# Second attention of an encoder layer: value loads that wait for an exponential, transposes called earlier, thirteen units without copies

## The chip, the cores and the metric

The kernel runs on one core of one Trainium2 chip. The metric is the device time of one execution in microseconds (us). Times before the change are the median of three runs and one profiled execution of the same program.

## The reference: one encoder layer on two sequences

Two sequences of 2048 tokens and width 1024 go through one layer with shared weights. An input projection yields queries, keys, values and gates of two attention branches. Branch A is windowed attention (8 query heads, 2 key heads). Branch B, which the change touches, is neighbourhood attention: the tokens form a grid of 32 rows by 64 columns, and each query sees a window of 8 rows by 16 columns. Both are gated, concatenated, projected out and added to the input, and a gated side path is added. Cut to branch B:

```python
def neighbourhood_attn(q, k, v, rpb):
    ...
    def row(r):
        ...
        sc = jnp.einsum('bnqhd,banchd->bnhqac', qr, kb).astype(jnp.float32) * scale
        ...
        sc = jnp.where(mask, sc + bias.astype(jnp.float32), -jnp.inf)
        sc = sc.reshape(b, NA_N_COL_BLOCKS, B_HEADS, NA_COL_BLOCK, wr * NA_KEY_COLS)
        pr = jax.nn.softmax(sc, axis=-1)
        pr = pr.reshape(b, NA_N_COL_BLOCKS, B_HEADS, NA_COL_BLOCK, wr, NA_KEY_COLS).astype(vb.dtype)
        o = jnp.einsum('bnhqac,banchd->bnqhd', pr, vb)
        return o.reshape(b, GRID_W, B_WIDTH)
```

## The kernel before

Products that need accuracy split each fp32 operand into a high and a low part of type fp32r and run three matmuls (`project`: high x high, high x low, low x high).

**Stages.** The program has 96 units `f`. Units 0 to 31 are the tiles of branch A. Units 32 to 95 are branch B: `divmod` splits `f - 32` into a half of the heads (32 to 63 and 64 to 95), a sequence and a tile `j` of 16, which is a block of 8 grid rows `b` and of 16 columns `cb`. Its 128 queries see 288, 384, 360 or 480 keys, by `j`, in 3 or 4 chunks (`window`, `chunks`); units with `j` = 5, 6, 9, 10 are the wide ones (480 keys, 4 chunks), those with `j` = 0, 3, 12, 15 the narrow ones (288). After unit 95 follow the output projection and the side path.

**What TensorE does in a unit.** Beside the attention of unit `f` run the projections of a tile six ahead (`stream`, `proj_b`: pqk for queries and keys, pvg for values and gates, 24 matmuls each, at 215 ns by the planner's count, 10320 a unit). The table `PLAN_B` says at which share of the unit's projection each step of the attention is called: the four score products (`sc`, tile scb), the exponentials (`exp`), the preparation of the next queries (`prep`), four times the transposes (`pt`, tile ptb), and four times the product with the values (`po`, tile pob), of which the last two are called in the next unit (second number 0). The order on TensorE is pinned to the order of the calls; on the other engines and on SP's queue a scheduler orders the instructions, unless `P` pins them.

**The way of the exponentials.** DVE adds the bias to the scores and takes the maximum (`softmax`, s, mx), ACT takes the exponential in place in the order of heads 0, 2, 1, 3 (`exps`). The transposes are cheaper in fp32r. So a DMA on ACT's queue copies each head's exponentials from s to tn, a tile of type fp32r (L310), and `pt` transposes tn. If `exps` gets no tile `turned`, there is no copy and `pt` transposes s as fp32. Before, the last six units (90 to 95) do that. The transposed probabilities are split into high and low part by ACT (p_t, L935) and DVE (L936); the products pob go through an addition otb (ACT L954, DVE L955) to the output.

**Loads on SP's queue.** SP issues its DMAs in order. In each unit these are the values vw (`load_values`, three or four loads, L903, called with `exp`), the store of the output (ob_d, L964), the biases of the next unit that has new ones (L888), stores of projected values (v_d, L846) and the next tokens (stx, L361). In units 56 and 57 SP also loads the weights of the second half of heads (wa and wb, eight times 512 KB each, L197), in units 88 and 89 the first weights of the next stage (L1013). The biases wait for the last exponential of the unit before (`last_ex`, through `after`). The scratch buffers that the steps share are small rings: `sc` (3 PSUM banks, for scores, transposes and gates), s (5) and p_t (3).

Of the kernel before, what the change touches and what calls it, by code (L numbers as in the profile page):

```python
# [11 lines left out]
F32 = mybir.dt.float32  # L12
# [46 lines left out]
def bias_offsets():  # L59
# [39 lines left out]
PLAN_B = (  # L99
    (0.00, 1, "sc", 0), (0.03, 1, "sc", 1), (0.07, 1, "sc", 2), (0.09, 0, "po", 2), (0.11, 1, "sc", 3), (0.16, 0, "po", 3),  # L100
    (0.16, 1, "exp", 0), (0.24, 0, "fin", 0), (0.35, 1, "prep", 0),
    (0.68, 1, "pt", 0), (0.75, 1, "pt", 1), (0.82, 1, "pt", 2), (0.86, 1, "po", 0), (0.90, 1, "pt", 3), (0.95, 1, "po", 1),
)


def emit(ctx, tc, io):
# [179 lines left out]
    def after(ins, other):  # L286

        tc.add_manual_dep(ins.ins, other.name, mybir.DependencyInfo(mybir.DependencyClass.Sync, mybir.DependencyReason.DATA),
                          reason="behind the copies")

    def exps(sm, fct, gs, sink=None, turned=None):

        mx, nm, den, rd, ss = (sm[k] for k in ("mx", "nm", "den", "rd", "s"))
        if sink is None:
            nc.vector.tensor_scalar_mul(nm, mx, -1.0)
            yield
        else:
            nc.vector.scalar_tensor_tensor(out=nm, in0=mx, scalar=-1.0, in1=sink[1], op0=ALU.mult, op1=ALU.min)  # L298
        waiting = []
        for n_, i in enumerate((0, 2, 1, 3) if sink is None else range(4)):  # L300
            ex = nc.scalar.activation(ss[i], ss[i], AF.Exp, bias=nm[:, i:i + 1], accum_out=den[:, i:i + 1])  # L301
            if sink is None:
                last_ex[:] = [ex.ins]
            if sink is None and (n_ == 0 or turned is not None):
                P(ex)
            if sink is None and turned is not None:
                waiting.append(i)
                for k in waiting[:1] if n_ in (1, 2) else waiting[:] if n_ == 3 else ():
                    to = turned[:, k, :ss[k].shape[-1]]
                    P(nc.scalar.dma_start(to.bitcast(F32), ss[k]))  # L310
                    ss[k] = to
                    waiting.remove(k)
        if sink is not None:
            es = ap.tile([128, 4], F32, tag="es", name="es", bufs=3)
            nc.vector.tensor_tensor(out=es, in0=sink[0], in1=nm, op=ALU.add)
            nc.scalar.activation(es, es, AF.Exp)
            yield
            behind(nc.vector.tensor_tensor(out=den, in0=den, in1=es, op=ALU.add))
            nc.vector.reciprocal(out=nm, in_=den)
            nc.gpsimd.tensor_copy(rd, nm)  # L320
            nc.gpsimd.tensor_copy(rd[0:64, 1::2], nm[64:128, 0::2])
            nc.gpsimd.tensor_copy(rd[64:128, 0::2], nm[0:64, 1::2])
        else:
            nc.vector.reciprocal(out=rd, in_=den)
        nc.gpsimd.tensor_scalar_mul(rd, rd, fct)
        g2 = ap.tile([128, 4, HD], F32, tag="g2", name="g2", bufs=2)
        nc.gpsimd.tensor_tensor(out=g2, in0=gs.rearrange("p (h d) -> p h d", h=4),
                                in1=rd.unsqueeze(2).broadcast_to([128, 4, HD]), op=ALU.mult)
        sm["g2"] = g2.rearrange("p h d -> p (h d)")
        yield  # L330
# [540 lines left out]

    bt = []

    def unit_b(f):
        half, st = divmod(f - 2 * NT, 2 * NT)
        s, j = divmod(st, NT)
        b, cb = divmod(j, 4)
        _, gs = held[f]
        r0, nr, c0, ncol, rows = window(b, cb)
        kc, ch = rows * ncol, chunks(nr, rows)  # L880
        nch, kn = len(ch), [ncol * n for _, n in ch]
        n = nr * ncol
        if cb != 2:
            off, _ = BIAS_OFF[(row_type(b), col_type(cb))]
            if not bt:
                bt.append(big([128, 2, 4, 512], F32, "bias"))
            bt.append(bt[0][:, len(bt) % 2])
            load = nc.sync.dma_start(bt[-1][:, :, :n],  # L888
                                     io["bias"][half][:, off:off + 4 * n].rearrange("p (h n) -> p h n", h=4))
            if last_ex:  # L890
                after(load, last_ex[0])
        bias = bt[-1]
        vw = []

        def load_values():

            spare = f >= 6 * NT - 6 and f % 2 == 0
            if spare:
                four = ap.tile([128, 4, 4, 2 * HD], F32R, tag="raw", name="vw4", bufs=1)
            for j in range(nch):  # L900
                v = four[:, j] if spare else \
                    ap.tile([128, 4, 2 * HD], F32R, tag=("vp", "vr_")[j % 2], name="vw", bufs=3 - j % 2)
                nc.sync.dma_start(v[:kn[j]].bitcast(F32).rearrange("p h d -> p (h d)"),  # L903
                                  v_d[half, s, cb][r0 + ch[j][0]:r0 + sum(ch[j])]
                                  .rearrange("r c h a d -> (r c) (h a d)"))
                vw.append(v)

        sees = [query_rows(b, cb, j) for j in range(nch)]
        order = sorted(range(nch), key=lambda j: sees[j][1] - sees[j][0])
        at = [16 * sum(z - a for a, z in sees[:j]) for j in range(nch + 1)]  # L910
        sm, p_ts, got = sm_tiles(), [], {}

        def sc(h):
            ps = ptile([128, 512], "sc", "scb")
            for j, q in enumerate(qs[f]):
                mm(ps[:, :n].rearrange("p (r c) -> p r c", c=ncol), q[h % 2][:, 128 * (h // 2):128 * (h // 2) + 128],
                   ks_b[h % 2][:, r0:r0 + nr, h // 2, c0:c0 + ncol], j == 0, j == 1)
            softmax(h, ps, n, bias[:, h, :n], sm)
            if h == 3:
                if not tn:  # L920
                    tn.append(ap.tile([128, 4, 480], F32R, tag="ev", name="tn", bufs=1))
                got["ex"] = exps(sm, hr_b[:, st:st + 1], gs, turned=tn[0] if f < 6 * NT - AHEAD - 1 else None)
                next(got["ex"])

        def pt(x):
            h = (0, 2, 1, 3)[x]
            pt = ptile([128, 512], "pt", "ptb")
            for j in order:

                c = at[j] - 16 * sees[j][0]  # L930
                k0 = ncol * ch[j][0]
                tr(pt[:kc, c:c + 128], sm["s"][h][:, k0:k0 + kc], rowwise)
            p_t = main.tile([128, 2, 512], F32R, tag="p_t", name="p_t", bufs=3)
            hi, lo, pf = p_t[:kc, 0, :at[-1]], p_t[:kc, 1, :at[-1]], pt[:kc, :at[-1]]
            nc.scalar.copy(hi, pf)  # L935
            nc.vector.tensor_tensor(out=lo, in0=pf, in1=hi.bitcast(F32), op=ALU.subtract)  # L936
            p_ts.append(p_t)

        def po(x):
            h = (0, 2, 1, 3)[x]  # L940
            e, i = h % 2, h // 2
            if i == 0:
                got["po"] = ptile([128, 2, 256], "ms", "pob")
            if x == 0:
                got["ot"] = ap.tile([128, 2, 2, 128], F32, tag="ot", name="otb", bufs=2)
            po, ot = got["po"], got["ot"]
            for j in order[::-1]:
                a, z = sees[j]
                mm(po[:, i, :].rearrange("p (a q) -> p a q", a=2)[:, :, 16 * a:16 * z], vw[j][:kn[j], h, :],
                   p_ts[x][:kn[j], :, at[j]:at[j + 1]], j == order[-1], j == order[0])  # L950
            if i == 1:
                a, z = 64 * e, 64 - 64 * e
                pq = po.rearrange("p i (a q) -> p i a q", a=2)
                nc.scalar.copy(ot[a:a + 64], pq[z:z + 64])  # L954
                nc.vector.tensor_tensor(out=ot[a:a + 64], in0=pq[a:a + 64], in1=ot[a:a + 64], op=ALU.add)  # L955

        def fin(_):
            pgt = ptile([128, 2, 128], "sc", "pgtb")
            for i in range(2):
                tr(pgt[:, i, :], sm["g2"][:, 128 * i:128 * i + 128], rowwise)  # L960
            o_t = ap.tile([128, 2, 128], F32, tag="o_t", name="o_tb", bufs=2)
            nc.gpsimd.tensor_tensor(out=o_t, in0=got["ot"][:, :, 0], in1=got["ot"][:, :, 1], op=ALU.add)
            nc.vector.tensor_tensor(out=o_t, in0=pgt, in1=o_t, op=ALU.mult)
            nc.sync.dma_start(ob_d[s][b, :, 2 * half:2 * half + 2, cb, :], o_t)  # L964
        return {"sc": sc, "pt": pt, "po": po, "fin": fin, "prep": lambda _: nxt(f),
                "exp": lambda _: (next(got["ex"]), load_values())}


# [500 lines left out]
```

## Time and profile before

| what | us |
|---|---|
| median of three runs | 2490.5 (2489.25 to 2492.84) |
| the profiled execution | 2492.04 |
| its span, first to last instruction | 2490.3 |
| first attention, 0 to 806.70 | 806.70, TensorE busy 793.95 |
| second attention, units 32 to 89, 806.70 to 1757.45 | 950.75, TensorE busy 928.56 |
| units 90 to 95, 1757.45 to 1841.00 | 83.55, TensorE busy 81.58 |
| output projection and side path, 1841.00 to the end | 649.30, TensorE busy 643.39 |

The page gives shares of the span by engine. In its second part the digits are tenths of busy time in 40 slices of the span; the DMA line is the mean busy share of the core's 16 DMA engines.

```profile
PEclk9999999999999999999999999999999999999999
DMA  6422233322354677767967787777977455756765
GB/s 208 134 97 94 88 103 98 97 94 87 102 178 153 203 252 234 232 210 228 336 217 228 225 266 255 244 247 266 316 232 272 163 171 175 265 176 217 242 227 170
```

Slices are 62.3 us wide. In the second attention (slices 13 to 28) the DMA engines are busy between 60% and over 90%; the highest rate, 336 GB/s, falls on the slice from 1183 to 1245 us, in units 55 to 58. In the third part, q1 is SP's queue and q10 is ACT's, which carries hardly anything but the copies to tn:

```profile
q1 hardware_dynamic: 245376, 437.84, 54.1%
q10 hardware_dynamic: 33696, 45.09, 5.3%
```

### The profile page before, as it was taken

What the parts mean: (1) busy time and instruction counts of PE and PEld (TensorE: products, weight loads), DVE (VectorE), ACT (ScalarE), POOL (GpSimd) and SP (SyncE); (2) the same over time, 40 slices, a digit from 0 to 9 for tenths busy, and PEclk for the clock granted to TensorE, in tenths of its full rate; (3) what the DMA queues carried; (4) which work ended last, traced back from release to release, by engine and by line L of the source; (5) the groups of instructions that cost most, each with busy time, mean ns of one, the idle gap of its engine ahead of it and who ended that gap; (6) DMA issues with size and microseconds to landing.
All of it is one profiled execution on the core that took longest, in us unless ns stands there. A gap on an engine that the chain in (4) does not pass through costs nothing. (4 is left out here: it accounts for less than half of the span.)

```text
span 2490.3 us, 40934 instructions
## 1 busy us (share of the span) xinstructions
PE 2447.5 (98%) x13062; PEld 2060.5 (83%) x13062; DVE 1705.6 (68%) x4215; ACT 1412.8 (57%) x3408; POOL 853.1 (34%) x1363
## 2 busy tenths in 40 slices
PE   8999999999999999999899999999999999999999
PEld 7888888888888888888778888887777888888887
DVE  6777777777765666666566666776537655686776
ACT  6777777777764665665456566665663222354443
POOL 4555555555543544554344444443110000000000
PEclk9999999999999999999999999999999999999999
DMA  6422233322354677767967787777977455756765
GB/s 208 134 97 94 88 103 98 97 94 87 102 178 153 203 252 234 232 210 228 336 217 228 225 266 255 244 247 266 316 232 272 163 171 175 265 176 217 242 227 170
DMA packets 279288, 485.55 MB, mean 195 GB/s; under 512 B 31617, under 2 KB 120097, under 8 KB 274849
## 3 DMA queue, kind: packets, MB, share of 16 engines
q1 hardware_dynamic: 245376, 437.84, 54.1%
q10 hardware_dynamic: 33696, 45.09, 5.3%
q8 instruction: 104, 1.70, 0.3%
q14 instruction: 112, 0.91, 0.1%
HBM read 307.72 MB, written 134.23 MB: 177 GB/s over the span
## 5 line engine op out<-in xcount | busy, mean ns | idle before, releaser
L258 PE MATMUL pqk<-wa,xr 128*128 128x512 f32 x1536 | 452.5, 411 | 0.0
L258 PE MATMUL pvg<-wb,xr 128*128 128x512 f32 x1536 | 450.6, 406 | 0.0
L301 ACT ACTIVATE s<-s,nm 128x320 f32<-128x320 f32 (+6 forms) x512 | 293.5, 575 | 131.1 <-DVE nm L298 119.1
L258 PEld LDWEIGHTS pvg<-wb,xr 128*128 128x128 f32 x1536 | 272.5, 190 | 34.1
L1254 ACT CAST opd<-raw 128x512 fp32r<-128x512 f32 x224 | 131.7, 619 | 270.6 <-PE acca L1272 117.9
L258 PEld LDWEIGHTS pqk<-wa,xr 128*128 128x128 f32 x1536 | 257.1, 188 | 29.7
L379 POOL TENSOR_TENSOR xr<-stx,xr 128x512 fp32r<-128x512 f32 x186 | 238.6, 1296 | 107.5 <-ACT xr L378 77.7
L1255 DVE TENSOR_TENSOR opd<-raw,opd 128x512 fp32r<-128x512 f32 x224 | 146.6, 686 | 145.6 <-ACT opd L1254 145.6
L258 PE MATMUL pg<-wb,xr 128*128 128x512 f32 x768 | 233.0, 409 | 1.0 <-DVE vv L536 1.0
L258 PE MATMUL pq<-wa,xr 128*128 128x512 f32 x768 | 219.3, 400 | 0.0
L954 ACT COPY otb<-pob 64x512 f32<-64x512 f32 x128 | 74.5, 582 | 213.3 <-PE pob L258 213.1
L936 DVE TENSOR_TENSOR p_t<-ptb,p_t 128x368 fp32r<-128x368 f32 (+5 forms) x256 | 121.6, 487 | 91.3 <-ACT p_t L935 88.7
L1272 PE MATMUL accc<-opd,wb 128*128 128x512 f32 x768 | 177.0, 389 | 0.5 <-DVE r L1317 0.5
L1272 PE MATMUL acca<-opd,wa 128*128 128x512 f32 (+1 forms) x780 | 176.2, 386 | 0.8 <-ACT r L1350 0.5
L1272 PE MATMUL acca<-opd,s 128*128 128x512 f32 x768 | 175.4, 389 | 0.0
L1272 PEld LDWEIGHTS acca<-opd,wa 128*128 128x128 f32 x780 | 144.9, 188 | 30.9 <-ACT ev L1050 0.8
L1272 PEld LDWEIGHTS accc<-opd,wb 128*128 128x128 f32 x768 | 144.1, 188 | 30.8 <-DVE r L1317 1.0
L1272 PEld LDWEIGHTS acca<-opd,s 128*128 128x128 f32 x768 | 144.2, 188 | 29.9
L143 POOL TENSOR_TENSOR yb<-vrb,power 128x8 f32<-128x8 f32 x64 | 106.5, 1664 | 175.7 <-DVE vrb L813 158.0
L935 ACT CAST p_t<-ptb 128x368 fp32r<-128x368 f32 (+5 forms) x256 | 107.5, 427 | 86.5 <-PE ptb L262 74.6
L258 PEld LDWEIGHTS pob<-p_t,vw 128*128 128x128 f32 (+2 forms) x832 | 132.6, 189 | 24.6 <-DVE p_t L936 4.4
L258 PEld LDWEIGHTS pq<-wa,xr 128*128 128x128 f32 x768 | 135.1, 189 | 17.3
(174 smaller groups left out, 5188.1 us busy)
## 6 DMA issues: line engine op xcount, KB each, us to landing
stx<-x_b SPq DMA_DIRECT2D x128, 256.0 KB
vw<-v_d SPq DMA_DIRECT2D x96, 256.0 KB
stx<-x_a SPq DMA_DIRECT2D x64, 256.0 KB
stn<-x_n SPq DMA_DIRECT2D x64, 256.0 KB
v_d<-vb SPq DMA_DIRECT2D x64, 256.0 KB
ple_d<-ev SPq DMA_DIRECT2D x64, 256.0 KB
xres<-x_r SPq DMA_DIRECT2D x64, 256.0 KB
x_d<-r SPq DMA_DIRECT2D x64, 256.0 KB
```

The lines of the kernel that those rows point to most:

```text
L143: nc.gpsimd.tensor_tensor(out=y, in0=v, in1=power.broadcast_to([128, n]), op=ALU.pow)
L258: pinned(nc.tensor.matmul(out, lhsT, rhs, start=start, stop=stop))
L301: ex = nc.scalar.activation(ss[i], ss[i], AF.Exp, bias=nm[:, i:i + 1], accum_out=den[:, i:i + 1])
L379: low.tensor_tensor(out=lo, in0=raw, in1=hi.bitcast(F32), op=ALU.subtract)
L935: nc.scalar.copy(hi, pf)
L936: nc.vector.tensor_tensor(out=lo, in0=pf, in1=hi.bitcast(F32), op=ALU.subtract)
L954: nc.scalar.copy(ot[a:a + 64], pq[z:z + 64])
L1254: P(nc.scalar.copy(hi, v))
L1255: P(nc.vector.tensor_tensor(out=lo, in0=v, in1=hi.bitcast(F32), op=ALU.subtract))
L1272: pinned(nc.tensor.matmul(ps[:, cols], w[k][:, a, c:c + 128], o[:, b, cols], start=i in (0, 1, 4) and k == 0 and j == 0, stop=k == 3 and j ...
```

## The change

Four edits. In `PLAN_B` the transposes 0 to 2 are called earlier (0.60, 0.68, 0.76), the last one later (0.94), and the first two products with the values later (0.91 and 0.98). The value loads of a unit that copies wait for that unit's second exponential. A new function `copied_` names the units that copy: all but 55 to 58 and 87 to 95, so that 13 units transpose in fp32 instead of 6. The biases wait for the last exponential of the unit before only if that unit and their own both copy.

```diff
@@ -99,7 +99,7 @@
 PLAN_B = (
     (0.00, 1, "sc", 0), (0.03, 1, "sc", 1), (0.07, 1, "sc", 2), (0.09, 0, "po", 2), (0.11, 1, "sc", 3), (0.16, 0, "po", 3),
     (0.16, 1, "exp", 0), (0.24, 0, "fin", 0), (0.35, 1, "prep", 0),
-    (0.68, 1, "pt", 0), (0.75, 1, "pt", 1), (0.82, 1, "pt", 2), (0.86, 1, "po", 0), (0.90, 1, "pt", 3), (0.95, 1, "po", 1),
+    (0.60, 1, "pt", 0), (0.68, 1, "pt", 1), (0.76, 1, "pt", 2), (0.91, 1, "po", 0), (0.94, 1, "pt", 3), (0.98, 1, "po", 1),
 )
@@ -300,7 +300,7 @@
             if sink is None:
-                last_ex[:] = [ex.ins]
+                last_ex[:] = last_ex[-3:] + [ex.ins]
@@ -871,6 +871,10 @@
+    def copied_(f):
+
+        return not (4 * NT - 9 <= f < 4 * NT - 5 or f >= 6 * NT - 9)
+
@@ -887,8 +891,8 @@
-            if last_ex:
-                after(load, last_ex[0])
+            if f > 2 * NT and copied_(f) and copied_(f - 1):
+                after(load, last_ex[-1])
@@ -900,9 +904,11 @@
-                nc.sync.dma_start(v[:kn[j]].bitcast(F32).rearrange("p h d -> p (h d)"),
+                load = nc.sync.dma_start(v[:kn[j]].bitcast(F32).rearrange("p h d -> p (h d)"),
...
+                if copied_(f):
+                    after(load, last_ex[1])
                 vw.append(v)
@@ -919,7 +925,7 @@
-                got["ex"] = exps(sm, hr_b[:, st:st + 1], gs, turned=tn[0] if f < 6 * NT - AHEAD - 1 else None)
+                got["ex"] = exps(sm, hr_b[:, st:st + 1], gs, turned=tn[0] if copied_(f) else None)
```

On TensorE, in the middle of an ordinary unit (unit 34; pktb are transposes of the keys, pqk the projection, ptb the transposes of the exponentials, x3 one head's), the difference reads:

```order
 L264 MATMUL pktb<-ident,kb 128x128 x2
 L258 MATMUL pqk<-wa_9501,xr 128x512 x3
-L258 MATMUL pqk<-wa_9503,xr 128x512 x3
+L258 MATMUL pqk<-wa_9503,xr 128x512 x2
+L262 MATMUL ptb<-rowwise,tn 128x128 x3
+L258 MATMUL pqk<-wa_9503,xr 128x512
 L258 MATMUL pqk<-wa_9505,xr 128x512 x3
 L262 MATMUL ptb<-rowwise,tn 128x128 x3
 L258 MATMUL pqk<-wa_9507,xr 128x512 x3
+L258 MATMUL pqk<-wa_9509,xr 128x512
 L262 MATMUL ptb<-rowwise,tn 128x128 x3
```

The first head's transposes stand behind 5 products of pqk instead of 9, the second's behind 9 instead of 12, and the third's (not shown) behind 13 instead of 16.

On DVE, from the end of unit 33 to the first softmax of unit 34 (p_t is the low part of the transposed probabilities, ssqb the sum of squares of the projection, otb the addition behind the second product with the values; s,mx the softmax), before:

```order
L936 TENSOR_TENSOR p_t<-ptb,p_t 128x320 x4
L955 TENSOR_TENSOR otb<-pob,otb 64x512
L810 TENSOR_REDUCE ssqb<-sqb 128x8
L277 ISA s,mx<-scb,bias 128x384
L277 ISA mx 128x1
L813 TENSOR_SCALAR vrb<-ssqb,ep_b 128x8
```

and in the changed kernel:

```order
L942 TENSOR_TENSOR p_t<-ptb,p_t 128x320 x3
L810 TENSOR_REDUCE ssqb<-sqb 128x8
L961 TENSOR_TENSOR otb<-pob,otb 64x512
L813 TENSOR_SCALAR vrb<-ssqb,ep_b 128x8
L277 ISA s,mx<-scb,bias 128x384
L277 ISA mx 128x1
```

The addition moves behind the sum of squares, and the first softmax behind both and behind vrb. 16 of the 64 units have this order; in the others the first softmax stands ahead of the addition.

On SP's queue, in unit 56, the end of the weight loads wa and the biases of unit 57 (128x4x480) before:

```order
L197 DMA wa_15570<-sp_1wa_214 128x1024
L197 DMA wa_15572<-sp_1wa_215 128x1024
L197 DMA wa_15574<-sp_1wa_216 128x1024
L197 DMA wa_15576<-sp_1wa_217 128x1024
L888 DMA bias<-bias 128x4x480
L846 DMA v_d_309<-vb 8x8x512
```

and in the changed kernel, where the first two of the eight weight loads are the last rows shown:

```order
L907 DMA vw<-v_d_308 120x512 x2
L892 DMA bias<-bias 128x4x480
L970 DMA ob_d_92<-o_tb 128x2x128
L846 DMA v_d_308<-vb 8x8x512
L846 DMA v_d_309<-vb 16x8x512
L846 DMA v_d_310<-vb 8x8x512
L639 DMA raw<-w_gate 128x1024 x2
L361 DMA stx<-x_b 128x512 x2
L197 DMA wa_15554<-sp_1wa_210 128x1024
L197 DMA wa_15556<-sp_1wa_211 128x1024
```

The biases move from behind all eight weight loads to ahead of them. The biases of unit 89 move in the same way, ahead of the weight loads of unit 88.

More of the change, by code (lines that the diff above doesn't have):

```diff
@@ L902, in load_values @@
                     ap.tile([128, 4, 2 * HD], F32R, tag=("vp", "vr_")[j % 2], name="vw", bufs=3 - j % 2)
-                nc.sync.dma_start(v[:kn[j]].bitcast(F32).rearrange("p h d -> p (h d)"),
-                                  v_d[half, s, cb][r0 + ch[j][0]:r0 + sum(ch[j])]
-                                  .rearrange("r c h a d -> (r c) (h a d)"))
+                load = nc.sync.dma_start(v[:kn[j]].bitcast(F32).rearrange("p h d -> p (h d)"),
+                                         v_d[half, s, cb][r0 + ch[j][0]:r0 + sum(ch[j])]
+                                         .rearrange("r c h a d -> (r c) (h a d)"))
+                if copied_(f):
+                    after(load, last_ex[1])
                 vw.append(v)
```

## The prediction, as it stood before the result

> **What bounds the kernel now.** I read the page first: TensorE is busy nearly all the time, so the kernel shortens only where TensorE waits or where work is taken from it.
>
> ```profile
> PE 2447.5 (98%) x13062; PEld 2060.5 (83%) x13062; DVE 1705.6 (68%) x4215; ACT 1412.8 (57%) x3408; POOL 853.1 (34%) x1363
> ```
>
> The second view is TensorE's waits, asked stretch by stretch over the second attention (first score products of units 32 to 90 at 806.70 and 1757.45 us). The columns are the total, the number of waits and the longest one.
>
> ```profile
> PE ptb L262 <- DMA tn<-s: 2.9, 4, 1.1
> ```
> ```profile
> PE ptb L262 <- DMA tn<-s: 9.1, 8, 3.1
> PE scb L258 <- DVE mx L277: 1.1, 1, 1.1
> ```
> ```profile
> PE ptb L262 <- DMA tn<-s: 2.9, 5, 1.0
> ```
> ```profile
> PE scb L258 <- DVE mx L277: 2.5, 1, 2.5
> PE pple L258 <- DVE qg L850: 1.8, 1, 1.8
> PE ptb L262 <- DMA tn<-s: 0.9, 1, 0.9
> ```
>
> These are units 32 to 54 (800 to 1174.64), 55 to 60 (to 1285.49), 61 to 87 (to 1717.24) and 88, 89 (to 1757.45). Nearly all waiting is for one thing: the ACT queue's copies of the exponentials (tn<-s), which the transposes read. Half of it lies in six units.
>
> A wait shows less than it costs, so the third view compares stretches whose units have the same shapes. The columns are the stretch, its length, each engine's busy us, then the granted clock, the DMA share and GB/s.
>
> ```profile
> 917.91:1015.59 97.68, 96.41 (x535) 80.31 (x534) 64.42 (x162) 57.99 (x139) 47.76 (x55) 1.00 0.72 234
> 1174.64:1285.49 110.85, 100.32 (x535) 80.95 (x534) 64.03 (x162) 57.98 (x139) 45.22 (x53) 0.98 0.88 289
> 1191.92:1251.12 59.20, 52.40 (x273) 41.88 (x272) 32.94 (x81) 29.70 (x70) 24.83 (x28) 0.97 0.95 328
> 1460.57:1510.63 50.06, 49.45 (x273) 40.97 (x272) 34.62 (x84) 31.99 (x73) 20.00 (x24) 1.00 0.77 256
> 1460.57:1492.97 32.40, 32.40 (x179) 26.90 (x178) 22.78 (x56) 21.16 (x49) 13.33 (x16) 1.00 0.77 254
> 1717.24:1757.45 40.21, 34.77 (x179) 28.19 (x178) 23.47 (x57) 20.81 (x49) 8.22 (x12) 0.96 0.89 316
> ```
>
> Units 39 to 44 take 97.68 us and units 55 to 60 take 110.85: 13.2 more for matmuls of the same shapes. Units 72, 73 take 32.40, units 88, 89 take 40.21: 7.8 more. With the 2.9 + 2.9 of the other units, some 27 us can be won at most, about 1.1% of the time.
>
> **Term 1, units 55 to 60 (fp32 transposes in 55 to 58).** Here two sets of weights are reloaded and the DMA engines are full (share 0.95 in units 56 to 58). The queues of those 59.20 us:
>
> ```profile
> q1 hardware_dynamic: 7350, 16.66, 81.3%
> q10 hardware_dynamic: 1728, 2.70, 13.6%
> ```
>
> Without the copies (q10) SP's queue needs 0.813 x 59.20 = 48.1 us, and the same three shapes, undisturbed, take 50.06. So transfers just fit behind TensorE, with nothing to spare. Besides, the biases of unit 57 stand behind eight weight loads on SP, are issued 14 us into unit 56, and hold up the first softmax of unit 57:
>
> ```profile
> 1206.22 0.38 SPq L888 DMA_DIRECT2D bias<-bias  x1
> ```
> ```profile
> 1215.89 0.66 DVE L277 CUSTOM_DVE_ANT_0 s<-scb,bias 128x480 f32<-128x480 f32 x1 [0.93 <-DMA bias<-bias]
> ```
>
> The order moves them ahead of all eight, which takes away the 1.1 us score wait. I take 10.5 of the 13.2: unit 59 copies again while SP's queue is still working off its backlog, and the last six loads of wb still stand behind stores of v_d that wait for data. What is late next, if anything, is a weight. Ends: 7 (gaps on the DMA engines eat the room and more) and 13.2.
>
> **Term 2, units 87 to 89.** The same two things go: the copies, and the biases of unit 89 behind the weights of the next stage.
>
> ```profile
> 1739.10 0.66 DVE L277 CUSTOM_DVE_ANT_0 s<-scb,bias 128x480 f32<-128x480 f32 x1 [2.06 <-DMA bias<-bias]
> ```
>
> The late biases make the scores late, those the exponentials, and those the 1.8 us wait of pple. I take 6.0 of 7.8 (ends 4 and 7.8). Both long idles also cost clock afterwards:
>
> ```profile
> 1205.40:1208.90 3.50, 3.50 (x14) 2.82 (x14) 1.75 (x4) 1.89 (x4) 2.91 (x2) 0.51 1.00 353
> 1741.30:1744.80 3.50, 3.50 (x11) 2.70 (x10) 1.92 (x6) 3.40 (x9) 0.73 (x1) 0.51 0.77 222
> ```
>
> The granted clock is 0.51 for 3.5 us after an idle of 3.1 us and one of 2.5 us: 1.7 us of work lost each, already inside 13.2 and 7.8. [...]
>
> **Term 3, the other units: values' loads behind the second exponential.** In unit 38 (from 899.77), SP, ACT and TensorE:
>
> ```profile
> 904.17 1.75 SPq L903 DMA_DIRECT2D vw<-v_d  x4
> ```
> ```profile
> 905.89 0.47 ACTq L310 DMA_DIRECT2D tn<-s  x1
> 906.35 0.19 ACT L301 ACTIVATION_READ_ACCUMULATOR s<-s,nm 128x1 f32 x1
> ```
> ```profile
> 911.98 0.54 PE L262 MATMUL ptb<-rowwise,tn 128*128 128x128 f32 x4 [1.09 <-DMA tn<-s]
> ```
>
> Four loads (up to 256 KB each by their tiles) are issued ahead of the first copy, which is then read 6.1 us after its issue, 1.09 late. With the wait they start at 906.35 + 0.19 = 906.5, 2.4 us later and behind the copy. On SP the store of ob and the next biases stand behind them and move about 1.2 us; the biases' reader is the first softmax of unit 39 (from 917.91, the first row of the stretches), still 9 us on. The values are read by pob, which follows these transposes, so 7.8 us after their first issue or later; pob itself moves two matmuls on, and the values lose about 2 of at least 7.8. I take 4.8 of 2.9 + 2.9 (ends 2 and 5.8).
>
> [...]
>
> **Costs.** Seven more units transpose in fp32 (12 or 16 transposes each). Four transposes, fp32r and then fp32:
>
> ```profile
> 1749.20 0.45 PE L262 MATMUL ptb<-rowwise,tn 128*128 128x128 f32 x4
> 1749.49 0.93 PE L258 MATMUL pple<-p_r,wa 128*128 128x512 f32 x3
> ```
> ```profile
> 1766.62 0.60 PE L264 MATMUL ptb<-rowwise,s 128*128 128x128 f32 x4
> 1766.98 0.94 PE L258 MATMUL pple<-p_r,wa 128*128 128x512 f32 x3
> ```
>
> From start to next start 0.29 and 0.36: 0.07 more a head, 7 x 4 x 0.07 = **2.0**.
>
> In 16 units the order puts the otb addition ahead of the first softmax. The rows of unit 66 (from 1363.09) on DVE and ACT, the page's row of the otb copy, and the fourth score product of unit 67 (from 1378.82):
>
> ```profile
> 1363.39 0.68 DVE L955 TENSOR_TENSOR otb<-pob,otb 64x512 f32<-64x512 f32 x1 [0.49 <-ACT otb L954]
> 1364.02 0.69 DVE L810 TENSOR_REDUCE ssqb<-sqb 128x8 f32<-128x512 f32 x1
> 1364.62 0.55 DVE L277 CUSTOM_DVE_ANT_0 s<-scb,bias 128x384 f32<-128x384 f32 x1
> ```
> ```profile
> 1363.39 0.60 ACT L808 ACTIVATE sqb<-pqk 128x512 f32<-128x512 f32 x1
> ```
> ```profile
> L954 ACT COPY otb<-pob 64x512 f32<-64x512 f32 x128 | 74.5, 582 | 213.3 <-PE pob L258 213.1
> ```
> ```profile
> 1381.33 0.29 PE L258 MATMUL scb<-ks_b,q1b 128*128 128x288 f32 x1
> ```
>
> The second product now stands between the last pqk and the scores, so ACT can square 0.3 earlier, from 0.0 to 0.6 of the unit, and copies otb from 0.6 to 1.2. DVE reduces until 1.3, adds otb until 2.0, and after vrb the first softmax starts near 2.2 instead of 1.5. The fourth score product reuses the PSUM buffer of the first: in a narrow unit (288 columns) it comes at 2.5 and the buffer is free near 2.75. So 0.25 is missing in the 4 narrow units among the 16 and 0.1 in the 4 next wider ones: **1.4** (ends 0, and 6 if all 16 lose 0.35).
>
> Transposes 0 to 2 come earlier, in all 51 units that still copy:
>
> ```profile
> 1371.36 2.32 PE L258 MATMUL pqk<-wa,xr 128*128 128x512 f32 x9
> 1373.52 0.37 PE L262 MATMUL ptb<-rowwise,tn 128*128 128x128 f32 x3
> ```
> ```profile
> 1368.58 0.47 ACTq L310 DMA_DIRECT2D tn<-s  x1
> ```
> ```profile
> q10 hardware_dynamic: 240, 0.35, 34.0%
> ```
>
> Nine products take 2.16 us, so four are 0.96: the first transpose in unit 66 now comes 4.0 us after its copy's issue, not 4.9. The last row counts ACT's queue from 1368.58 to 1371.60: 3.0 us after the issue it had moved 0.35 MB, the first copy (192 KB) and most of the second, though the values went ahead. So the earlier read is covered in an ordinary unit. Ends: 0, and 51 x 0.96 = 49 if copies landed only just when they are read now. I take **1.7**, near the lower end. Transpose 3 comes two products later and wins time.
>
> **Sum.** -10.5 - 6.0 - 4.8 + 2.0 + 1.4 + 1.7 = -16.2 us. The profiled execution took 2492.04 (span 2490.3 and 1.7 around it), 1.5 above the median of the runs; 2492.04 - 16.2 - 1.5 = 2474.3.
>
> **Rivals.**
> - *Sharing remains* (0.15). The values run beside copies 1 to 3 instead of ahead of all four, and units 56 to 58 stay bound by transfers. For it: 48.1 of 50.06 leaves no room. Against: the waits begin mostly at the first copies. Half of terms 1 and 3 (15.3) goes: -16.2 + 7.7 = -8.5, 2482.0.
> - *Values or biases late* (0.12). They become the new wait in the wide units (480 columns, 12 that still copy), whose four loads, and in half of them biases, all move behind the exponentials. Against: no wait above names vw, and some 6 us are left. At 1 us in ten units: -6.2, 2484.3; with 4 us for weights late in units 57 and 58 as well, -2.2, 2488.3.
> - *Slower: transposes ahead of their copies* (0.10). The copies of ordinary units land later than 4.0 us after issue, because values now run beside the second and third. Place: the first three ptb of 51 units. Without my 1.7 the sum is -17.9, so from 0.35 us a unit (51 x 0.35 = 17.9) the gain is gone; at 0.6 the time is 2490.5 - 17.9 + 30.6 = 2503.2. For it: with four transposes a unit, any of them can be the late one. Against: the 0.35 MB within 3.0 us.
> - *The change doesn't do what it says* (0.03): the scheduler keeps the loads where they were. The order speaks against it.
>
> **Numbers.** My forecast (-9 to -24) has 0.60. A measurement tells about 0.2% (5 us) from no change. Faster by more: 0.60 + 0.14 (nearly all of the first rival) + 0.04 (a third of the second) = 0.78. Slower: 0.09 of the third. Within: the rest, 0.13. The range goes down to all that can be won less the fp32 cost, 2490.5 - 26.8 + 2.0 = 2465.7, and up over the first rival and half of the second, to 2487; some 0.2 is left out, nearly all of it above.
>
> **What would show it.** Right: units 55 to 60 near 100 us and 88, 89 near 34; no clock at 0.5 in the second attention; ptb's wait for tn under 5 us in all; vw issued after the second exponential. Wrong: waits of pob for vw, of scb for mx in the narrow units, or many short waits of ptb for tn between 61 and 86; in units 57 and 58 waits of pqk or pvg for their weights, if term 1 runs into the DMA engines.

## The result, and the profile after

The changed kernel takes 2484.05 us (median of 8 runs, 2482.03 to 2487.09) against 2491.41 (2488.98 to 2492.89) for the kernel before beside it: ratio 0.9972, 95% interval 0.9961 to 0.9982. It is 7.4 us faster, where 16.2 were forecast: the time lies inside the stated range, at its upper end, and the sum is off by 8.8. The profiled execution took 2484.0 us (span 2482.2), 8.1 below the span of before, so the profile can account for it.

The page first: engines, then granted clock, DMA share and rate of the 40 slices, then the queues of SP and ACT.

```profile
PE 2445.7 (99%) x13062; PEld 2063.1 (83%) x13062; DVE 1699.0 (68%) x4215; ACT 1411.2 (57%) x3408; POOL 851.0 (34%) x1363
```
```profile
PEclk9999999999999999999999999999999999999999
DMA  6422232322354667667966687778867455756765
GB/s 208 137 95 94 88 103 95 100 94 88 103 179 131 219 231 240 232 211 248 304 201 227 223 263 252 245 249 273 289 229 274 163 169 174 269 174 215 243 227 170
```
```profile
q1 hardware_dynamic: 245376, 437.84, 53.4%
q10 hardware_dynamic: 29664, 39.19, 4.7%
```

The copies of seven units are gone (q10 moves 39.19 MB, not 45.09), SP's queue moves the same, and the busiest slice falls from 336 to 304 GB/s. Now TensorE's largest waits of the second attention, stretch by stretch as in the prediction: units 32 to 54, 55 to 60, 61 to 86, 87 to 89, and 90 to 95.

```profile
PE ptb L262 <- DMA tn<-s: 3.0, 4, 2.2
```
```profile
PE ptb L262 <- DMA tn<-s: 1.6, 2, 1.5
PE pvg L258 <- DMA wb<-sp_1wb: 0.3, 1, 0.3
```
```profile
PE ptb L262 <- DMA tn<-s: 6.0, 10, 0.9
```
```profile
PE pple L258 <- ACT ev L1056: 0.7, 1, 0.7
```
```profile
PE scb L258 <- DVE p_t L942: 3.8, 1, 3.8
```

The large waits of 55 to 60 and 87 to 89 are gone. Those of the units that copy all along were to vanish and have grown from 5.8 us in all to 9.0, and a wait of 3.8 us stands where there was none. The lengths of the same stretches, before (the first, third and last) and after (all, with units 90, 91 and then unit 92); the columns are those of the prediction's stretches.

```profile
806.73:1174.65 367.92, 364.61 (x2018) 304.74 (x2017) 244.72 (x620) 221.80 (x528) 181.48 (x205) 1.00 0.72 228
...
1285.50:1701.32 415.82, 412.92 (x2284) 344.56 (x2283) 284.74 (x718) 263.78 (x615) 183.91 (x216) 1.00 0.75 240
...
1786.03:1799.84 13.81, 13.78 (x76) 10.96 (x75) 7.34 (x21) 9.94 (x25) 2.45 (x5) 1.00 0.94 298
```
```profile
806.51:1178.41 371.90, 367.46 (x2017) 305.73 (x2016) 242.49 (x620) 220.71 (x528) 181.18 (x205) 1.00 0.70 230
1178.41:1278.19 99.78, 97.72 (x536) 81.34 (x536) 63.55 (x163) 59.15 (x139) 45.11 (x52) 1.00 0.82 268
1278.19:1697.79 419.60, 413.59 (x2285) 344.30 (x2284) 281.86 (x719) 261.96 (x615) 182.80 (x216) 1.00 0.73 242
1697.79:1747.58 49.79, 49.10 (x269) 41.06 (x268) 33.93 (x86) 31.12 (x72) 15.50 (x21) 1.00 0.83 273
1747.58:1775.69 28.11, 28.11 (x160) 23.95 (x160) 16.15 (x41) 20.03 (x46) 4.88 (x10) 1.00 1.00 322
1775.69:1794.27 18.58, 14.79 (x75) 12.34 (x74) 7.07 (x21) 10.36 (x26) 2.42 (x5) 0.91 0.87 304
```

Units 55 to 60 went from 110.85 to 99.78 and 87 to 89 from 56.14 to 49.79, together -17.4. Units 32 to 54 lost 4.0, 61 to 86 lost 3.8, unit 92 lost 4.8; 90, 91 and 93 to the end gained 0.5 and 2.5 (why is left open). This is one profile of each kernel: in a second one of the changed kernel (h1 below) the ordinary units lost 1.9 and 2.5. So the experiments have two questions: why the ordinary units got worse instead of better, and what happens in unit 92.

The stall of unit 92 on ACT and TensorE:

```profile
1778.63 0.58 ACT L1056 COPY ev<-pple 128x512 f32<-128x512 f32 x1 [4.05 <-DMA ple_d<-ev]
```
```profile
1780.88 0.61 PE L258 MATMUL scb<-ks_b,q1b 128*128 128x288 f32 x1 [3.79 <-DVE p_t L942]
```

ACT copies pple's result out of PSUM into a buffer whose earlier content is still being stored (ple_d<-ev on SP's queue). On ACT the high part p_t comes behind this copy (at 1779.63), on DVE the low part behind that (1780.37), and on TensorE the score product that needs their PSUM buffer (1780.88). The product that waits names DVE; the cause is a store. By the kernel's rings it is the one that SP issued at 1770.57, 8.1 us before the copy could go. Before, the same copy started 5.0 us after its store (issued at 1780.68) and waited for nothing:

```profile
1785.63 0.59 ACT L1050 COPY ev<-pple 128x512 f32<-128x512 f32 x1
```

### The profile page after: what moved, and what is told of

It is laid out like the page before. It is cut to its first block, busy times and chain, and to the rows that moved or that the text cites. A ratio compares the mean times of both kernels' runs of the same rounds, so it can differ in the third digit from the quotient of the medians.

```text
span 2482.2 us, 40847 instructions
## 1 busy us (share of the span) xinstructions
PE 2445.7 (99%) x13062; PEld 2063.1 (83%) x13062; DVE 1699.0 (68%) x4215; ACT 1411.2 (57%) x3408; POOL 851.0 (34%) x1363
## 3 DMA queue, kind: packets, MB, share of 16 engines
q10 hardware_dynamic: 29664, 39.19, 4.7%
## 5 line engine op out<-in xcount | busy, mean ns | idle before, releaser
L258 PE MATMUL pqk<-wa,xr 128*128 128x512 f32 x1536 | 442.7, 411 | 0.0
L258 PEld LDWEIGHTS pqk<-wa,xr 128*128 128x128 f32 x1536 | 262.1, 189 | 35.0
```

Source lines behind the costliest of these rows:

```text
L258: pinned(nc.tensor.matmul(out, lhsT, rhs, start=start, stop=stop))
```

## The experiments

Each run has five rounds beside the kernel before. Lengths of stretches are those between first score products, from each run's trace, against the one profile of before. They are one execution each: between the changed kernel and its second profile (h1) units 32 to 54 differ by 2.1 us and 61 to 86 by 1.3, and g3, whose instructions there are those of before, is 2.0 and 3.2 shorter than before. Less than that is not read from a single profile.

**e1: the old plan in the changed kernel.**

```diff
-    (0.60, 1, "pt", 0), (0.68, 1, "pt", 1), (0.76, 1, "pt", 2), (0.91, 1, "po", 0), (0.94, 1, "pt", 3), (0.98, 1, "po", 1),
+    (0.68, 1, "pt", 0), (0.75, 1, "pt", 1), (0.82, 1, "pt", 2), (0.86, 1, "po", 0), (0.90, 1, "pt", 3), (0.95, 1, "po", 1),
```

> The changed kernel with the old table PLAN_B (transposes at 0.68, 0.75, 0.82, products at 0.86, 0.95). Theory A (the transposes are now called ahead of their copies, because the values' loads share the DMA engines with copies 2 to 4): units 61 to 86 lose the 3.8 us that they gained in length, unit 52 stalls less (about 1.2 instead of 2.2 us), and the time is 2478 to 2481. Theory B (the values behind the second exponential cost by themselves, the places of the transposes do not matter): 2483 to 2486, the waits of ptb for tn stay near 10 us in all.

Measured 2480.47 us, ratio 0.9962 (0.9949 to 0.9975). The time is theory A's, the profile only half: units 32 to 54 are 1.6 over before instead of 4.0, but 61 to 86 still 3.1. By this run the plan is at most a part of the loss; its interval overlaps that of the changed kernel.

**e2: the biases' wait put back.** `ends` holds each unit's last exponential.

```diff
-            if f > 2 * NT and copied_(f) and copied_(f - 1):
-                after(load, last_ex[-1])
+            g = next((g for g in (f - 1, f - 2) if g >= 2 * NT and copied_(g)), None)
+            if g is not None:
+                after(load, ends[g])
```

> The changed kernel, but the biases of units 55, 56, 87 and 88 wait for the last exponential of the last unit before them that copies (54 or 86), as before. Theory A (the biases of 55 and 87, which wait for nothing, are issued three units early, at 3.9 us into units 52 and 84, right ahead of those units' copies, and make the stalls there): the 2.2 us wait and the half clock of unit 52 go, units 52 and 84 return to 16.0 us, and the time is 2484 - 3.5 - 1.0 = 2479 to 2481. Theory B (units 52 and 84 stall because of the values or the plan): 2483 to 2485, with the stall of unit 52 still there.

Measured 2478.02 us, 0.9952 (0.9939 to 0.9966), a little below theory A's range. Unit 84 is where it can be read. SP's queue there in the changed kernel, and TensorE's transposes:

```profile
1650.05 0.38 SPq L892 DMA_DIRECT2D bias<-bias  x1
1652.13 1.35 SPq L907 DMA_DIRECT2D vw<-v_d  x3
```
```profile
1656.28 0.43 PE L262 MATMUL ptb<-rowwise,tn 128*120 128x128 f32 x3 [0.50 <-DMA tn<-s]
1657.56 0.36 PE L262 MATMUL ptb<-rowwise,tn 128*120 128x128 f32 x3
1659.45 0.41 PE L262 MATMUL ptb<-rowwise,tn 128*120 128x128 f32 x3 [0.54 <-DMA tn<-s]
```

The bias row is the bias of unit 87 (0.7 MB): nothing holds it back any more, and its buffer is free after unit 84's last softmax, so it goes three units early, straight ahead of unit 84's copies. With the wait the unit takes 15.60 us instead of 17.08 and its transposes wait for nothing. In unit 52 theory A was wrong: without the early bias it still took 17.35.

**e3: the values behind the last exponential.**

```diff
-                    after(load, last_ex[1])
+                    after(load, last_ex[3])
```

> The changed kernel, but the values wait for the unit's last exponential instead of the second. Theory A (the values' share of the DMA engines makes copies 2 to 4 late): copies 2 and 3 land up to 1 us earlier, the waits of ptb for tn fall from 10.6 to under 5 us, and the time is 2478 to 2481. Theory B (the values are now the late ones: they are issued 1.3 us later and pob reads them 6 us on): new waits of pob for vw in the wide units and 2484 to 2490.

Measured 2483.06 us, 0.9968 (0.9955 to 0.9981): no gain that can be measured, between the two theories. The profile is of one of its fastest runs (2479.05). The waits of units 32 to 89:

```profile
PE pob L258 <- DMA vw<-v_d: 3.9, 11, 0.6
PE scb L258 <- DVE mx L277: 1.4, 2, 1.0
PE ptb L262 <- DMA tn<-s: 0.7, 1, 0.7
```

Both mechanisms are there: the copies are no longer late (0.7 us in place of 10.6), and the values are.

**e4: no wait of the values.** The two lines `if copied_(f):` and `after(load, last_ex[1])` go.

> The changed kernel without the values' wait (the loads go as soon as SP reaches them). Theory A (with the transposes called 0.9 us earlier the wait is needed, since the first copies would land 0.8 us later): the waits of ptb for tn double to 20 us or more and the time is 2490 to 2498. Theory B (the wait is worth nothing, only moves the collision from copy 1 to copies 2 and 3): 2482 to 2486.

Measured 2500.04 us, 1.0037 (1.0023 to 1.005), slower than before and beyond theory A's range: with the transposes called early the wait is worth 16 us.

**f1: units 87 to 89 copy again.**

```diff
-        return not (4 * NT - 9 <= f < 4 * NT - 5 or f >= 6 * NT - 9)
+        return not (4 * NT - 9 <= f < 4 * NT - 5 or f >= 6 * NT - 6)
```

> The changed kernel, but units 87 to 89 copy again (and their values and biases wait accordingly), so that the second block of fp32 units is 90 to 95 as before. Theory A (what units 87 to 89 gain is given back: TensorE reaches units 91 and 92 some 6 us earlier, where the DMA engines are full anyway, so that ACT's copies of pple wait for their stores): units 87 to 89 are 5 to 6 us longer, the 3.8 us wait of unit 92 and its half clock go (unit 92 back to 13.8 us), and the time is 2484 to 2487. Theory B (unit 92 stalls for a reason of its own): the stall stays, and the time is 2489 to 2491.

Measured 2491.69 us, 1.0003 (0.9994 to 1.0012): the time is just above theory B's range. But unit 92's wait shrank from 3.8 to 1.2 us, and in the profile (of the fastest run, 2486.92) the time was lost in units 87 to 89 themselves, 15.3 us over the changed kernel: the biases of unit 89, which wait again here, were late and held TensorE up for 6.3 us. The run moves two things and does not decide.

**f2: loads of wb moved back by passes.**

```diff
-            if m % 4 == 3 and (n < 3 or m == 3):
+            if m % 4 == 3 and (n > 1 or m == 3):
```

> The changed kernel, with two of the eight loads of the weights wb (512 KB each) moved from the first two passes of pple to the third and fourth, so behind unit 92. Theory A (the DMA engines are full from 1757 to 1781 us, and the stores of pple, for which ACT waits in unit 92, are late by their backlog): 1 MB at some 380 GB/s is 2.7 us less, the wait of unit 92 falls from 3.8 to about 1 us, without half a clock, and the time is 2478 to 2481. Theory B (the stores are late for another reason than the amount of traffic): unit 92 keeps its 3 to 5 us, 2483 to 2485.

Measured 2482.51 us, 0.9966 (0.9954 to 0.9979), with 4.4 us of wait in unit 92. The edit missed its aim: between 1757 and 1775 us SP issued three loads of wb, as many as in the changed kernel. It says nothing on the traffic.

**f3 and f4: only the 13 units, without and with the values' wait.** e2's kernel with the old plan; f3 also leaves out the wait of e4.

> Of the change only the 13 units without copies remain: the old PLAN_B, no wait of the values, and the biases wait for the last unit that copies (as in e2_bias_back). Theory A (terms 1 and 2 are the whole gain: -11.1 in units 55 to 60, -6.4 in 87 to 89, +4.8 in unit 92, -2.5 behind it; the values' wait and the new plan together bring nothing): 2475 to 2478, no more than e2_bias_back's 2478. Theory B (the values' wait with the new plan brings the 4.8 us of term 3): 2481 to 2484.

> The same with the values' wait: 13 units without copies, biases that wait for the last copying unit, values behind the second exponential, the old PLAN_B. Theory A (the values' wait helps only where the transposes are not called earlier; copies 2 and 3 then have 0.6 to 0.9 us more until they are read): the waits of ptb for tn fall below 4 us and the time is 2473 to 2476, less than e2_bias_back and less than f3_old_plan_no_wait. Theory B (the wait shifts the collision from copy 1 to copies 2 and 3 under either plan): as f3_old_plan_no_wait, within 2 us.

Measured 2477.54 (0.9948, 0.9934 to 0.9962) and 2477.20 us (0.9945, 0.9932 to 0.9957). Theory A of f3 and theory B of f4 hold: under the old plan the values' wait is worth nothing that can be measured (an estimate from the scatter of their runs: 2 us either way, so 4.8 would show), and 13 units without copies are the whole gain. In the profiles f4 waits less for copies than f3 (ptb for tn 5.0 us against 9.0 in units 32 to 89), but for values as well (pob for vw 1.4 against none). Unit 52, where f4 is the slower one, shows how the wait can cost. Three times 4 us from its first score product, without the wait (f3) and with it (f4); the last columns are clock, DMA share and GB/s.

```profile
1125.57:1129.57 4.00, 4.00 (x24) 3.64 (x23) 3.49 (x12) 0.87 (x2) 0.21 (x1) 1.00 0.79 303
1129.57:1133.57 4.00, 4.00 (x20) 3.20 (x20) 2.73 (x5) 3.16 (x9) 3.40 (x3) 1.00 0.79 241
1133.57:1137.57 4.00, 4.00 (x23) 3.29 (x22) 2.79 (x6) 3.59 (x9) 3.00 (x5) 1.00 1.03 324
```
```profile
1123.64:1127.64 4.00, 4.00 (x24) 3.63 (x23) 3.50 (x12) 0.87 (x2) 1.66 (x1) 1.00 0.85 330
1127.64:1131.64 4.00, 4.00 (x20) 3.19 (x20) 1.72 (x5) 3.16 (x9) 2.38 (x4) 1.00 0.38 102
1131.64:1135.64 4.00, 3.44 (x18) 2.51 (x16) 1.57 (x4) 1.71 (x4) 0.93 (x2) 1.00 1.03 269
```

And the second and third head's transposes of f4's unit 52:

```profile
1135.90 0.43 PE L262 MATMUL ptb<-rowwise,tn 128*120 128x128 f32 x3 [0.82 <-DMA tn<-s]
1137.75 0.40 PE L262 MATMUL ptb<-rowwise,tn 128*120 128x128 f32 x3 [0.41 <-DMA tn<-s]
```

While the values are held back, the DMA engines have little to do: 102 instead of 241 GB/s, so 0.56 MB less in 4 us; over the 49 units that copy all along, the fifth to eighth us of a unit have 98 GB/s in f4 and 218 in f3, by the packets. Then values and copies 2 to 4 come together at full load, and the second and third copy are late; in f3 no transpose of this unit waits.

**g1: all loads of wb behind unit 92.** f4 and:

```diff
-            if m % 4 == 3 and (n < 3 or m == 3):
+            if m % 2 and n > 2:
                 load_coming()
...
-            nc.sync.dma_start(w.bitcast(F32), parts_d[key])
+            load = nc.sync.dma_start(w.bitcast(F32), parts_d[key])
+            if n == 1:
+                after(load, last_ex[-1])
```

> f4_old_plan_wait with all eight loads of the weights wb (4 MB) moved behind unit 92: they are issued in the fourth and fifth pass of pple and wait for an exponential there. (In f2_wb_later SP still issued three of them between 1757 and 1775 us, as many as in the changed kernel, so that run left the traffic of that stretch as it was.) Theory A (backlog: the stores of pple stand behind more loads than the DMA engines move, and ACT waits for a store): three to four loads less ahead of unit 92 are 1.5 to 2 MB, 4 to 5 us at some 380 GB/s; the 3.9 us wait and the half clock of unit 92 go, unit 92 takes about 14 us, and the time is 2477.2 - 5 = 2471 to 2474. Theory B (not the traffic): unit 92 stays at 18 to 20 us, 2476 to 2479. If the weights come late instead, the output projection begins with a wait for wb.

Measured 2472.21 us (4 runs, 2468.46 to 2474.07), 0.9917 (0.9904 to 0.993): theory A. Unit 92 takes 13.61 us, and TensorE does not wait in it. The 20 us ahead of the place of the stall, in the changed kernel and in g1:

```profile
1757.00:1777.00 20.00, 20.00 (x117) 17.00 (x115) 10.79 (x27) 13.92 (x32) 3.23 (x7) 1.00 1.05 350
```
```profile
1745.50:1765.50 20.00, 20.00 (x116) 16.57 (x116) 11.74 (x28) 15.63 (x36) 2.98 (x7) 1.00 0.84 277
```

With the DMA engines at 0.84 instead of full (1.05 as this view counts), the stores land in time. The output projection begins without a wait for wb. But full engines alone don't make the stall; the same stretch of the kernel before, which had none:

```profile
1766.00:1786.00 20.00, 20.00 (x116) 16.54 (x115) 11.34 (x28) 15.06 (x35) 3.99 (x9) 1.00 1.00 337
```

There the store landed in time, but with little to spare: in g3, which leaves this stretch as before, ACT waited 1.0 us for it.

**g2: the new plan alone.** The kernel before with the changed line of PLAN_B.

> The kernel before with the new PLAN_B alone. Theory A (without the values' wait the transposes are called ahead of their copies: e4_no_wait lost 9.3 us in units 32 to 54 and 13.4 in 61 to 86): 15 to 25 us slower than before, 2506 to 2516, with 25 us or more of waits of ptb for tn. Theory B (what e4_no_wait lost came from the early biases of units 55 and 87 and from the missing wait together, not from the places of the transposes): at most 5 us slower.

Measured 2506.0 us, 1.0063 (1.0051 to 1.0076): slower, as theory A has it. The waits of units 32 to 89:

```profile
PE ptb L262 <- DMA tn<-s: 27.4, 24, 2.5
```

In the profile, of a run 6 us above the median, units 32 to 54 are 6.1 longer than before and 61 to 86 8.4. Unit 92 is 6.1 longer too, although 87 to 89 here take as long as before: there the new plan alone brings the stall.

**g3: only the biases of units 57 and 89 without their wait.** The kernel before, with

```diff
-            if last_ex:
+            if last_ex and f not in (4 * NT - 7, 6 * NT - 7):
```

> The kernel before, in which only the biases of units 57 and 89 no longer wait, so that they stand ahead of the weight loads on SP; all units copy as before. Theory A (the two late biases are the smaller part of term 1 and the larger part of term 2): units 55 to 60 lose the 1.05 us wait of scb and little else, units 87 to 89 lose the 2.5 us wait of scb, the 1.7 us of half clock and the 1.8 us wait of pple; 2491 - 7 = 2483 to 2486. Theory B (the DMA engines are full, so that what the biases gain the weights and copies lose): 2489 to 2492, with longer waits of ptb for tn in units 56 to 58 and 88, 89.

Measured 2488.45 us (12 runs, 2480.14 to 2497.55), 0.999 (0.9979 to 1.0): nothing certain. The profile is of the fastest run and no measure of the time, but it shows the kind of waits left in units 55 to 89:

```profile
PE ptb L262 <- DMA tn<-s: 8.7, 11, 1.9
PE pple L258 <- DVE qg L850: 2.1, 1, 2.1
```

The 3.6 us of waits for the two late biases are gone, the copies' waits remain. By the interval the two biases bring at most 5.2 us, where terms 1 and 2 measured 17.4 together. So the copies are the main part of them.

**h1 to h4: the changed kernel again, each pair of biases by itself, and the new plan on g1.** h2 lets e2's rule look at f - 1 only (biases 55 and 87 wait), h3 makes only those of 56 and 88 wait, h4 is g1 with the new PLAN_B.

> The changed kernel itself once more, as the reference of h2 and h3 on the same chip. Expected is 2484 within 1.5 us; its profile shows how far the stretches of units 32 to 54 and 61 to 86 differ between two executions of the same instructions (2 to 3 us each by g3 against the kernel before).

> The changed kernel, but only the biases of units 55 and 87 wait for the last exponential of 54 and 86; those of 56 and 88 wait for nothing. Theory A (it is the two loads issued three units early, ahead of the copies of units 52 and 84): 2478 to 2480, nearly all of e2_bias_back's 6 us. Theory B (it is the biases of 56 and 88): 2483 to 2485.

> The changed kernel, but only the biases of units 56 and 88 wait for the last exponential of 54 and 86; those of 55 and 87 wait for nothing. Theory A: 2482 to 2484. Theory B: 2478 to 2480.

> g1_wb_behind_92 with the new PLAN_B: values behind the second exponential, biases that wait for the last copying unit, wb behind unit 92. Theory A (the new places of the transposes bring nothing by themselves and cost 1 to 3 us): 2473 to 2476, above g1_wb_behind_92's 2472. Theory B (with the stalls by biases and tail gone, the later products and the fourth transpose pay): 2468 to 2471.

Measured 2482.93 (h1; 0.9968, 0.9957 to 0.9979), 2481.18 (h2; 0.9962, 0.995 to 0.9975), 2482.57 (h3; 0.9963, 0.9951 to 0.9976) and 2474.60 us (h4; 0.9935, 0.9921 to 0.9948). The intervals of h1 to h3 overlap, so the times do not tell the pairs apart: h2 falls between its theories, h3 into the range of its theory A. The lengths of single units separate, among the profiles with the new plan and the values behind the second exponential: with the early bias unit 84 took 16.67 to 17.29 us in four, without it 15.59 to 15.66 in four; unit 54 17.71 to 18.20 in five, without 16.80 to 17.17 in three; unit 86 17.40 to 19.17 in four, without 16.81 to 17.27 in four. By the medians that is some 1.4, 1.1 and 0.9 us, about 3.4 in all, shared by both pairs. Unit 52 does not separate (17.02 to 19.57 against 17.35 to 19.29). h4 is 2.4 above g1, inside theory A's range; their intervals overlap.

**i1: values last, products late.** g1 with `last_ex[3]`, and the products at 0.91 and 0.98, the fourth transpose at 0.94.

> g1_wb_behind_92 with the values behind the unit's last exponential, the first three transposes at their old places (0.68, 0.75, 0.82) and the products at the new ones (0.91, 0.98; the fourth transpose at 0.94). Theory A (copies 2 and 3 late by the values are what is left in units 32 to 54 and 61 to 86, and the products are late enough for the values): no waits of ptb for tn, waits of pob for vw under 2 us, copies as fast as in e3_values_last (1.9, 2.0, 2.6, 3.8 us), and 2468 to 2471 against g1_wb_behind_92's 2472.2. Theory B (the values are the next to be late, as in e3_values_last with 4.6 us of such waits): 2472 to 2476.

Measured 2474.19 us, 0.9934 (0.9916 to 0.9951): theory B. The waits of units 32 to 89:

```profile
PE pob L258 <- DMA vw<-v_d: 5.1, 15, 0.7
PE scb L258 <- DVE mx L277: 1.3, 2, 0.9
```

## Why the prediction was wrong in its sum

- **Term 1 held.** Forecast -10.5, with the fp32 cost of four units (1.1) -9.4; measured -11.1. Units 55 to 60 are 99.8 us long, "near 100", between 9.8 and 13.6 shorter than before in every run with these four units in fp32, and f3 shows that it needs neither plan nor wait. The weights are late by 0.3 us only, as "what is late next" said.
- **Term 2 held where it stands.** Forecast -6.0, with 0.8 of fp32 cost -5.2; measured -6.4, -6.3 to -6.9 in every run that has units 87 to 89 in fp32 (f3's -6.9 without plan or wait). What the sum lacks is a term behind it: some 30 us later unit 92 is 4.3 to 7.4 us longer than before in every one of these runs that has loads of wb ahead of it, which takes most of term 2 back. There the stores of pple are queued behind more loads than the DMA engines move (in the changed kernel share 1.05 and 350 GB/s in the 20 us ahead of it, and the copy could go only 8.1 us after the store was issued), and g1 shows that the loads of wb are needed for it (without them 0.84 and 277 GB/s, and no wait). What sets the stall off is not shown. It need not be term 2: the runs without copies in 87 to 89 also let the biases of 91, 92, 93 and 95 go early, and the new plan brings the same stall without either (g2); with those biases early and 87 to 89 copying (f1) 1.2 us of wait are left.
- **Term 3 failed; it is the step of the sum that went wrong, beside two costs that the sum lacks (unit 92 and, below, the biases).** It said "With the wait they start [...] 2.4 us later and behind the copy", and took the first copy's waiting time as won. f3 and f4 differ by that wait alone and take 2477.5 and 2477.2: worth 0.3, not 4.8. The wait moves the collision from the first copy to the next ones. TensorE's waits show it: of the 5.8 us that the ordinary units waited for copies before, 5.2 were the first head's; of the 9.0 in the changed kernel 5.6 are the second's and third's, and the first's 3.2 all fall in units 52, 84 and 86, which have an early bias ahead of their copies (next point but one). By the packets of ACT's queue, taken in order, 128 to a copy, the four copies needed 3.0, 3.1, 3.6 and 5.0 us from issue to last packet before (means over 49 units that copy all along), and 2.0, 3.3, 4.1 and 4.9 in the changed kernel: the first is 1.0 faster, the second and third are slower, and the DMA engines have little to do in between (108 GB/s in the fifth to eighth us of these 49 units, 206 before). f3 and f4 show the same pair by themselves: 2.8, 3.0, 3.5 and 5.0 without the wait, 1.9, 3.2, 4.0 and 5.0 with it. With the values behind all four (e3, i1), the copies need 1.8 to 1.9, 2.0, 2.6 and 3.8 to 3.9, and the values are late. So in the changed kernel copies 2 and 3, with values beside them, take 1.3 and 1.5 us longer than with the values behind them.
- **The cost of the earlier transposes was about right, in the company of the wait.** I took 1.4 and 1.7, 3.1 together. The pairs with the new and the old plan differ by 3.6 (the changed kernel and e1), 2.4 (h4 and g1) and 0.8 (e2 and f4); the intervals overlap in each pair, but all three have the same sign. Alone the plan costs 14 us (g2): of the rival "transposes ahead of their copies" the place was right, 0.30 us a unit over 49 units in g2's profile against its break-even of 0.35, and the values' wait pays for most of it. In the profile the signs said so: "many short waits of ptb for tn between 61 and 86", 10 of them, 6.0 us.
- **A cost was missing: the biases that lost their wait.** I priced only those of 57 and 89, which gain. Those of 55, 56, 87 and 88 lost it as well and went ahead of the copies of units 52, 54, 84 and 86. Units 54, 84 and 86 show 3.4 us; the medians of e2 against the changed kernel's two say 5 to 6, the ratios to the kernel before beside each 4 to 5. (The biases of 59, 91, 92, 93 and 95 lost the wait too; no run holds these back by themselves.) That term 3 brought nothing (4.8) and that these biases cost 3 to 6 accounts for about the 9.5 us between the forecast -1.7 for the ordinary units and the measured +7.8; in h1's profile it is +4.4, so 6.1 to account for.
- **fp32 transposes held:** 2.0 in all. In f3 units 55 and 56 take 16.10 and 15.76 us, and the same shapes that copied without a wait 15.72 (unit 43) and 15.54 (unit 40): 0.38 and 0.22 a unit, forecast 4 x 0.07.
- **Rivals.** "Sharing remains" gave 2482.0, next to the result, with half of the mechanism: values beside copies 2 to 4, but units 56 to 58 were not bound. That its number fits so well is in part luck. "Values late" came true in e3 and i1 only.

A version that beats both kernels came out of it: g1, 13 units without copies, biases that wait for the last copying unit, the old plan, and wb behind unit 92. It takes 2472.2 us, 0.9917 of before.

## What to carry to other kernels

Here, holding a load back until another had gone helped the one (the first copy, 3.0 to 2.0 us) and bunched the rest (the second and third, 3.1 to 3.3 and 3.6 to 4.1): look at the rate of the DMA engines while it is held, and at the last transfer of the group, not the first. Whoever makes a wait conditional should ask for each load that loses it how early its buffer is free: here the bias of unit 87 was issued in unit 84, three units early, and that unit took 17.08 us (15.60 in e2, where the bias waits). And where a later stage is bound by transfers, time won just ahead of it has to be followed to the next wait before it is counted: of the 6.4 us won in units 87 to 89, unit 92 took 4.8 back.

## What the runs showed of the hardware

The granted clock fell to 0.50 for 3.41 us behind some of TensorE's idles. In the two traces of before and after, between the first 30 us and the last 5, this stands behind four of them: idles of 3.09 and 2.51 us before (they ended at 1205.24 and 1739.83) and of 2.20 and 3.79 us in the changed kernel (1135.45 in unit 52 and 1780.88 in unit 92). The longest idle that it does not stand behind took 1.86 us (before, ended at 1263.64): over the next 3.41 us the clock was 1.00. So 2.20 us was enough here. What decides between these lengths is not shown.
